# Entry of the experts' loop re-ordered, and two low parts of the first norm moved to VectorE, in a one-core DeltaNet, HGRN2 and PEER layer

## Chip, cores and metric

One Trainium2 chip, one core of it. The metric is the device time of one execution in microseconds (us). Three runs of the kernel before gave 2094.04, 2093.02 and 2092.74 us, a median of 2093.02.

## Reference

```
h = rmsnorm(x, norm1); proj = h @ w_in                  # x: 512 x 1024 float32
y_a = gated_delta(q, k, v, beta, alpha) ... @ w_branch_a
y_b = hgrn2(f, i, q) ... @ w_branch_b
x  = x + (sigmoid(g_a) * y_a + sigmoid(g_b) * y_b) @ w_out
h2 = rmsnorm(x, norm2)
s  = (h2 @ w_pq) . sub_keys; top 16 of each half; best 16 of the sums per head; gate = softmax
h  = gelu(h2 . expert_u[idx]); x = x + sum_k gate_k * h_k * expert_v[idx_k]     # 128 x 128 experts
out = rmsnorm(x, final_norm)
```

## The kernel before

Every float32 product is made of three: a matrix is split into a high part rounded for TensorE and a low part, the rest (`w_split`, L485: ScalarE copies `raw` into `hi`, and another engine computes `lo = raw - hi`), and high·high, high·low and low·high are added in PSUM. Weights come in units of 128 x 1024 float32 (512 KB) through a pool of three buffers for each of `wraw`, `whi` and `wlo`. `w_raw(n)` issues the load of unit n on SyncE's queue; `w_cut(n)` splits it. The argument `eng` says who computes the low part: VectorE (`vec`), GpSimd (`gps`), or, with `None`, ScalarE writes minus the high part and GpSimd issues a DMA that adds the raw data to it.

All instructions of an engine run in the order in which the program wrote them (`in_order`, L292), and each DMA queue takes its issues in that order too.

**The first norm (L1034 to L1093).** TensorE multiplies the unscaled x by units 0 to 4 while the norm is still being computed. Unit 1 (PSUM tile `poB`) is followed by unit 2 (`pl`), then by units 3 and 4 in turns (`pl`, `mm`). Beside unit 1, `squares(k)` squares one eighth of x on ScalarE and VectorE adds it into `acc` (L436). After two pieces of unit 2, `token_scales` (L441) sums `acc` over the partitions on TensorE (`mA`); VectorE forms `r` (L444) and GpSimd takes its power -1/2 (L445). `spread_scales` (L447) multiplies the identity by `r` on VectorE (`rd`, four 128 x 128 tiles) and spreads it with TensorE (`mC`). Then x is scaled and split again (`scaled`, `resplit`), and the next unit of TensorE needs the new `hhi` and `hlo`. A few small constants (`late_constants`, L351) are computed in between on VectorE and ScalarE.

**The experts' loop (L1785 to L1835).** Of the 128 x 128 experts, block i has 128. For tokens 0 to 367 all experts are computed densely: `u_mm` is the product with the block's u (24 products of 368 columns, `h` in PSUM; blocks 0 to 29 before the loop, the others in it), `u_act` the gelu into `slots`, and `y_mm(i)` adds gate · h · v into six PSUM banks (18 products, `y`). For the other tokens GpSimd gathers rows of u and v by index (`gather`, 128 rows of 1024 float32 each; five buffers), and VectorE consumes them. The dense gates lie in HBM as `gD`, written in slots of 32 tokens from `stage` (L1588); the last slot has 16 valid tokens, and of its 128 columns 16 are written there and the other 112 at L1807. `g_load(i)` (L1690) reads the gates of four blocks (768 KB) back into one of two buffers in `stage`; the second of them lies on the memory from which L1807 writes.

The loop runs i = -3, -2, ..., 127. Iteration i issues the loads of v and u of block i + 3 (`v_load`, L1702, and `w_load`, called at L1801), prepares block i + 1 (`prep`, L1717) and computes block i. `prep(m)` makes on VectorE `hg` (gate times slot, L1728), high parts `vh`, `wh`, then the split of the u block (`us`), then the low parts `wl` (L1741) and `vl` (L1742). `y_part` multiplies wh·vh, wh·vl, wl·vh in this order. At L1805 GpSimd copies one number of the first gates, so that the first gathers wait for them.

```
            if 0 < i + GLEAD < P:                     # L1793, GLEAD = 5, GB = 4
                g_load(i + GLEAD, nc.scalar)
            if n < NU:                                # L1800, n = i + 3
                uraw[n] = w_load(I["eut"][n + NPRE])
            if n == 0:
                g_load(0, nc.sync)
                gps.tensor_copy(cut(8512, 1), gbs[0][:, 0, 0, 0:1])
            if n == 1:
                nc.sync.dma_start(gD[NA - 1][:, 16:], gt[0][:, 16:])
```

Called with i = -1, `g_load(4, nc.scalar)` is thus issued on ScalarE's queue ahead of all work of `prep(0)`.

Of the kernel before, what the change touches and what calls it, by code (L numbers as in the profile page):

```python
# [22 lines left out]
P = 128  # L23
T = 512
D = 1024
DC = D // P
# [17 lines left out]
NPRE = 30  # L44
# [29 lines left out]
NDMA = 4  # L74
# [5 lines left out]
GLEAD = 5  # L80
LAG = 2
GB = 4
# [197 lines left out]
def build(ctx, tc, I, O):  # L280
# [199 lines left out]
    def w_load(src):  # L480
        raw = wpool.tile([P, DC, UW], F32, tag="wraw", name="wraw")
        nc.sync.dma_start(raw, src)
        return raw

    def w_split(raw, eng=gps):  # L485
        hi = wpool.tile([P, DC, UW], F32R, tag="whi", name="whi")
        lo = wpool.tile([P, DC, UW], F32R, tag="wlo", name="wlo")
        act(hi, raw, AF.Copy)
        if eng is None:

            act(lo, hi.bitcast(F32), AF.Copy, scale=-1.0)
            gps.dma_start(out=lo, in_=raw, accum_op=OP.add)
        else:
            eng.tensor_tensor(lo, raw, hi.bitcast(F32), OP.subtract)  # L494
        return hi, lo

    def w_raw(n):
        if n < len(order):
            kind, j = order[n]
            raws[n] = w_load(I["eut"][j] if kind == "u" else I["wu"][UNITS[kind, j]])  # L500

    def w_cut(n):
        if n < len(order):
            wts[n] = w_split(raws.pop(n), vec if n < 2 else gps if n < N0 + NDMA else None)

    def piece(p, w, c, m):
        whi, wlo = w
# [8 lines left out]
    with ExitStack() as ph:  # L516
# [534 lines left out]
        for k in range((NF - 1) * DC):  # L1051
# [6 lines left out]
            if k < DC:  # L1058
                squares(k)
            if k == 1:  # L1060
                w_cut(3)
                w_raw(4)
            if k >= LB:
                next(lbs, None)
            if k == SC1:
# [574 lines left out]
    with ExitStack() as ph:  # L1640
# [76 lines left out]
        def prep(m, between=None):  # L1717
# [16 lines left out]
            else:  # L1734
                act(vh, vr, AF.Copy)
                act(wh, hg, AF.Copy)
            if m < NU:
                us[m] = w_split(uraw.pop(m), vec)
            if between is not None:
                consume(between, rws.pop(between))  # L1740
            vec.tensor_tensor(wl, hg, wh.bitcast(F32), OP.subtract)  # L1741
            vec.tensor_tensor(vl, vr, vh.bitcast(F32), OP.subtract)  # L1742
            vs[m], ws[m] = (vh, vl), (wh, wl)


# [39 lines left out]
        for i in range(-LEAD, P):  # L1785
            n = i + LEAD
            if i == P - TAIL - 1:
# [2 lines left out]
                nc.sync.dma_start(fn, I["fnorm"].partition_broadcast(P))  # L1790
                for tt in (NT,) + tuple(range(NT)):
                    x_load(tt)
            if 0 < i + GLEAD < P:  # L1793
                g_load(i + GLEAD, nc.scalar)
            if n < P - TAIL:
                v_load(n)
            if i == P - TAIL - EARLY - 1:
                for k in range(P - TAIL, P):
                    v_load(k)
            if n < NU:  # L1800
                uraw[n] = w_load(I["eut"][n + NPRE])  # L1801
            if n == 0:
                g_load(0, nc.sync)

                gps.tensor_copy(cut(8512, 1), gbs[0][:, 0, 0, 0:1])  # L1805
            if n == 1:
                nc.sync.dma_start(gD[NA - 1][:, 16:], gt[0][:, 16:])  # L1807
            if i == 8:
                sx = junk[:, 0:P].bitcast(I32)
# [58 lines left out]
```

## Time and profile before

| | |
|---|---|
| median of three runs | 2093.02 us |
| the profiled execution's own time | 2093.28 us |
| its span, first to last instruction | 2091.1 us |
| busy: TensorE | 2012.5 us (96%) |
| busy: VectorE / ScalarE / GpSimd | 1511.8 / 940.7 / 857.3 us |
| mean granted clock of TensorE | 0.990 |

The span is 2.2 us shorter than the time of the same execution. The shares are means over the whole span; the two places of the change are 20 us long each, so they are read in the timeline: there a row gives start, duration, engine and line, tiles, count, and in brackets how long the engine had been idle and what ended that. A row that merges several instructions gives their stretch from the first start to the last end.

### The profile page before, as it was taken

How to read it: one execution, taken by the hardware profiler on the slowest of the kernel's cores; microseconds unless marked ns; L12 is line 12 of the kernel's file. 1: busy time of each engine (PE TensorE's matmuls, PEld its weight loads, DVE VectorE, ACT ScalarE, POOL GpSimd, SP SyncE). 2: the span in 40 equal slices, each digit the busy share in tenths (PEclk: the TensorE clock that was granted, in tenths of full speed). 3: DMA queues.
4: the chain of work that ended last, by engine and by line, in shares of the span. 5: the costliest groups of instructions: out<-in, count | busy, mean ns of one | idle time of the engine just before them, and what ended most of it. 6: DMA issues, size and time to landing. Idle time of an engine off the chain costs nothing.

```text
span 2091.1 us, 34918 instructions
## 1 busy us (share of the span) xinstructions
PE 2012.5 (96%) x13182; PEld 1729.2 (83%) x13182; DVE 1511.8 (72%) x2956; ACT 940.7 (45%) x1739; POOL 857.3 (41%) x863
## 2 busy tenths in 40 slices
PE   7899999999999999999798899999999999999998
PEld 5678787887878787888787799999999998898886
DVE  7666546656662366999996587787877878788887
ACT  4555555545554323566575333333333333333334
POOL 3566645655645644311101134334334433334522
PEclk9999999999999999999999999999999999999999
DMA  3322232132222543677799799999989989889996
GB/s 134 114 72 83 64 107 73 62 98 63 83 83 93 191 156 126 186 199 192 192 331 330 281 330 327 337 319 332 327 321 326 325 323 324 320 327 323 323 312 228
DMA packets 194873, 456.84 MB, mean 218 GB/s; under 512 B 28128, under 2 KB 91776, under 8 KB 193040
## 3 DMA queue, kind: packets, MB, share of 16 engines
q1 hardware_dynamic: 96016, 231.29, 31.0%
q0 software_dynamic: 47520, 173.04, 26.3%
q10 hardware_dynamic: 51168, 50.28, 7.3%
q8 instruction: 103, 1.69, 0.3%
q14 instruction: 66, 0.54, 0.1%
HBM read 393.11 MB, written 39.40 MB: 207 GB/s over the span
## 4 chain that ended last, share of the span: by engine, by line
PE 58%; DVE 14%; ACT 2%; issue 2%; DMA 2%; POOL 0%; SPq 0%; ACTq 0%; DVEq 0%; POOLq 0%
PE y L285 23%; PE h L285 19%; PE mm L285 12%; DVE Bg L1564 2%; DVE stage L1266 1%; DVE scr L1262 1%; DVE stage L1260 1%; DVE A L1560 1%; PE iv L285 1%; DMA gD<-stage 1%; DVE oh L1314 1%; PE pl L285 1%; DVE tv L1258 1%; DVE tv L1264 1%; PE mC L285 1%
## 5 line engine op out<-in xcount | busy, mean ns | idle before, releaser
L494 POOL TENSOR_TENSOR wlo<-wraw,whi 128x1024 fp32r<-128x1024 f32 x106 | 255.0, 2407 | 269.3 <-ACT whi L288 268.8
L285 PE MATMUL h<-hhi,wlo 128*128 128x368 f32 x1024 | 339.4, 331 | 6.2 <-DMA wlo<-wraw 6.2
L285 PE MATMUL h<-hhi,whi 128*128 128x368 f32 x1024 | 340.4, 332 | 2.0 <-ACT hext L288 1.9
L285 PE MATMUL h<-hlo,whi 128*128 128x368 f32 x1024 | 339.5, 332 | 1.6 <-POOL hlo L459 1.2
L285 PE MATMUL mm<-hhi,whi 128*128 128x512 f32 x792 | 328.8, 415 | 1.0 <-ACT a_k L288 0.6
L285 PE MATMUL mm<-hlo,whi 128*128 128x512 f32 x792 | 311.4, 393 | 4.2 <-POOL hlo L459 3.0
L288 ACT ACTIVATE whi<-wraw 128x1024 fp32r<-128x1024 f32 (+1 forms) x251 | 263.2, 1049 | 110.7 <-PE mm L285 46.1
L285 PE MATMUL mm<-hhi,wlo 128*128 128x512 f32 x792 | 309.6, 391 | 2.0 <-DMA wlo<-wraw 2.0
L285 PE MATMUL y<-vl,wh 128*128 128x512 f32 x756 | 297.7, 394 | 10.8 <-DVE vl L1742 10.5
L285 PE MATMUL y<-vh,wh 128*128 128x512 f32 x756 | 295.5, 391 | 4.8 <-DVE wh L1733 4.8
L285 PE MATMUL y<-vh,wl 128*128 128x512 f32 x756 | 296.5, 392 | 0.0
L1660 POOL DMA_INDIRECT row<-eu,eidx x144 | 172.6, 1199 | 285.5 <-DVE stage L1670 271.9
L1660 POOL DMA_INDIRECT row<-ev,eidx x144 | 174.9, 1215 | 275.0 <-DVE h2g L1678 219.0
L494 DVE TENSOR_TENSOR wlo<-wraw,whi 128x1024 fp32r<-128x1024 f32 x99 | 121.3, 1225 | 177.3 <-ACT whi L288 175.7
L285 PEld LDWEIGHTS h<-hhi,wlo 128*128 128x128 f32 x1024 | 193.7, 189 | 12.0 <-DMA wlo<-wraw 7.7
L285 PEld LDWEIGHTS h<-hhi,whi 128*128 128x128 f32 x1024 | 193.2, 189 | 6.9 <-ACT hext L288 2.5
L285 PEld LDWEIGHTS h<-hlo,whi 128*128 128x128 f32 x1024 | 193.3, 189 | 2.5 <-POOL hlo L459 1.8
L288 ACT ACTIVATE hext<-h 128x368 f32<-128x368 f32 x88 | 41.9, 476 | 334.6 <-PE h L285 329.3
L285 PEld LDWEIGHTS mm<-hlo,whi 128*128 128x128 f32 x792 | 148.7, 188 | 40.1 <-POOL hlo L459 4.7
L285 PEld LDWEIGHTS y<-vl,wh 128*128 128x128 f32 x756 | 142.3, 188 | 43.2 <-DVE vl L1742 16.2
L285 PEld LDWEIGHTS mm<-hhi,whi 128*128 128x128 f32 x792 | 149.0, 188 | 27.7 <-ACT a_k L288 1.0
L285 PEld LDWEIGHTS mm<-hhi,wlo 128*128 128x128 f32 x792 | 149.4, 189 | 26.5 <-DMA wlo<-wraw 2.3
(443 smaller groups left out, 3758.4 us busy)
## 6 DMA issues: line engine op xcount, KB each, us to landing
wraw<-eut SPq DMA_DIRECT2D x128, 512.0 KB
stage<-ev SPq DMA_DIRECT2D x126, 512.0 KB
wraw<-wu SPq DMA_DIRECT2D x119, 512.0 KB
stage<-gD ACTq DMA_DIRECT2D x31, 768.0 KB
gD<-stage ACTq DMA_DIRECT2D x11, 2048.0 KB
wlo<-wraw POOLq DMA_DIRECT2D x42, 512.0 KB
sg<-sgD SPq DMA_DIRECT2D x16, 256.0 KB
sgD<-tmpP SPq DMA_DIRECT2D x14, 256.0 KB
```

What stands on the lines that cost most here:

```text
L285: nc.tensor.matmul(o, l, r, start=start, stop=stop)
L288: nc.scalar.activation(o, i, f, **kw)
L494: eng.tensor_tensor(lo, raw, hi.bitcast(F32), OP.subtract)
L1258: vec.max(val[:, 0:8], src)
L1260: vec.max_index(idx[:, 0:8], val[:, 0:8], src)
L1262: vec.match_replace(scr, val[:, 0:8], src, -3.0e38)
L1264: vec.max(val[:, 8:16], scr)
L1266: vec.max_index(idx[:, 8:16], val[:, 8:16], scr)
L1314: eng.tensor_tensor(oh[:, :, 0:n, :], oh[:, :, 0:n, :], oh[:, :, n:2 * n, :], OP.add)
L1560: vec.tensor_tensor(A, it[:, 0, t0:t0 + TB].rearrange("p (n u) -> p n u", u=2)[:, :, None, :].to_broadcast([P, TP, P, 2]), iov[:, None, :, ...
L1564: vec.tensor_tensor(Bg[:, q].rearrange("p n a b u -> p (n a) b u"), hi[:, p1:p1 + TP].rearrange("p n a u -> p (n a) u")[:, :, None, :].to_ ...
L1660: gps.indirect_dma_start(out=r, out_offset=None, in_=I["eu" if k < NK else "ev"], in_offset=bass.IndirectOffsetOnAxis(ap=at, axis=0))
```

## The change

At the start, the low part of unit 2 goes from GpSimd to VectorE; the split of unit 3 moves behind all eight squares and its low part to VectorE too. The last unit before the loop (the u block 29) has its low part computed by VectorE in place of ScalarE's copy and GpSimd's adding DMA. At the loop's entry, the first gates are loaded ahead of the first u block; GpSimd's copy writes into `gg2` instead of `stage`; the rest of the last gate slot is written one iteration later; `g_load(4)` is issued in iteration 1 instead of iteration -1; and in `prep(0)` the split of the u block stands behind `wl` and `vl`.

```
-            wts[n] = w_split(raws.pop(n), vec if n < 2 else gps if n < N0 + NDMA else None)
+            wts[n] = w_split(raws.pop(n), vec if n < 4 or n == len(order) - 1 else gps if n < N0 + NDMA else None)
...
             if k == 1:
+                w_raw(4)
+            if k == DC:
+
                 w_cut(3)
-                w_raw(4)
...
-            if m < NU:
+            if 0 < m < NU:
                 us[m] = w_split(uraw.pop(m), vec)
             if between is not None:
                 consume(between, rws.pop(between))
             vec.tensor_tensor(wl, hg, wh.bitcast(F32), OP.subtract)
             vec.tensor_tensor(vl, vr, vh.bitcast(F32), OP.subtract)
+            if m == 0:
+
+                us[m] = w_split(uraw.pop(m), vec)
...
-            if 0 < i + GLEAD < P:
+            if i == 1:
+                g_load(GB, nc.scalar)
+            elif GB < i + GLEAD < P:
                 g_load(i + GLEAD, nc.scalar)
...
+            if n == 0:
+                g_load(0, nc.sync)
+
+                gps.tensor_copy(gg2[:, 0:1], gbs[0][:, 0, 0, 0:1])
             if n < NU:
                 uraw[n] = w_load(I["eut"][n + NPRE])
-            if n == 0:
-                g_load(0, nc.sync)
-
-                gps.tensor_copy(cut(8512, 1), gbs[0][:, 0, 0, 0:1])
-            if n == 1:
+            if n == 2:
+
                 nc.sync.dma_start(gD[NA - 1][:, 16:], gt[0][:, 16:])
```

TensorE's instructions and their order are the same in both kernels. VectorE in the first norm, from the low part of unit 1 on (`wlo` low parts, `acc` the sums of squares, `mx` and `e` constants, `r` the scales), before:

```order
L494 TENSOR_TENSOR wlo<-wraw,whi 128x1024
L436 TENSOR_TENSOR acc<-acc,sq 128x512 x7
L355 TENSOR_TENSOR mx<-vecs 128x8
L356 TENSOR_TENSOR e_287<-vecs,mx 128x8
L357 TENSOR_TENSOR e_288<-vecs,mx 128x8
L444 TENSOR_SCALAR r_120<-mA 128x4
```

and now:

```order
L494 TENSOR_TENSOR wlo<-wraw,whi 128x1024 x2
L436 TENSOR_TENSOR acc<-acc,sq 128x512 x7
L494 TENSOR_TENSOR wlo<-wraw,whi 128x1024
L355 TENSOR_TENSOR mx<-vecs 128x8
L356 TENSOR_TENSOR e_287<-vecs,mx 128x8
L357 TENSOR_TENSOR e_288<-vecs,mx 128x8
L444 TENSOR_SCALAR r_120<-mA 128x4
```

One low part more stands ahead of the seven sums and one behind them, ahead of the constants and of `r`.

SyncE's queue at the loop's entry (`stage<-ev` a v block, `wraw<-eut` a u block, `stage<-gD` the first gates, `gD<-stage` the rest of the last gate slot), before:

```order
L1702 DMA stage<-ev 128x1024
L482 DMA wraw<-eut 128x1024
L1693 DMA stage<-gD 128x12x128
L1702 DMA stage<-ev 128x1024
L482 DMA wraw<-eut 128x1024
L1807 DMA gD<-stage 128x3584
L1702 DMA stage<-ev 128x1024
L482 DMA wraw<-eut 128x1024
```

and now:

```order
L1704 DMA stage<-ev 128x1024
L1695 DMA stage<-gD 128x12x128
L482 DMA wraw<-eut 128x1024
L1704 DMA stage<-ev 128x1024
L482 DMA wraw<-eut 128x1024
L1704 DMA stage<-ev 128x1024
L482 DMA wraw<-eut 128x1024
L1815 DMA gD<-stage 128x3584
```

The gates are second instead of third, and the write is behind the third pair of blocks instead of the second.

ScalarE there (`ogA<-h` and `hext<-h` gelus of u blocks, `whi` high parts of u blocks, `stage<-gD` the gates of blocks 4 to 7), before:

```order
L288 ACTIVATE ogA<-h 128x368 x4
L1693 DMA stage<-gD 128x12x128
L288 ACTIVATE whi<-wraw 128x1024
L288 ACTIVATE vh<-stage 128x1024
L288 ACTIVATE wh<-hg 128x384
L288 ACTIVATE whi<-wraw 128x1024
L288 ACTIVATE hext<-h 128x368
L288 ACTIVATE vh<-stage 128x1024
```

and now:

```order
L288 ACTIVATE ogA<-h 128x368 x4
L288 ACTIVATE whi<-wraw 128x1024
L288 ACTIVATE vh<-stage 128x1024
L288 ACTIVATE wh<-hg 128x384
L288 ACTIVATE whi<-wraw 128x1024
L1695 DMA stage<-gD 128x12x128
L288 ACTIVATE hext<-h 128x368
L288 ACTIVATE vh<-stage 128x1024
```

The load of the second gates has moved behind the high parts of u blocks 0 and 1 and of v block 1; it now stands ahead of the first gelu of the loop and of v block 2.

## Rows read from the trace of the kernel before

**Rows 1.** The page, busy time and share of the span by engine.
```profile
PE 2012.5 (96%) x13182; PEld 1729.2 (83%) x13182; DVE 1511.8 (72%) x2956; ACT 940.7 (45%) x1739; POOL 857.3 (41%) x863
```

**Rows 2.** Timeline of VectorE, first norm: start, duration (us), engine, line, tiles.
```profile
15.12 1.22 DVE L494 TENSOR_TENSOR wlo<-wraw,whi 128x1024 fp32r<-128x1024 f32 x1 [1.00 <-ACT whi L288]
17.45 4.80 DVE L436 TENSOR_TENSOR acc<-acc,sq 128x512 f32<-128x512 f32 x2 [1.11 <-ACT sq L288]
24.75 1.49 DVE L436 TENSOR_TENSOR acc<-acc,sq 128x512 f32<-128x512 f32 x2
26.16 0.16 DVE L355 TENSOR_TENSOR mx<-vecs 128x8 f32<-128x8 f32 x1
...
27.50 0.16 DVE L444 TENSOR_SCALAR r<-mA 128x4 f32<-128x4 f32 x1 [0.91 <-PE mA L285]
...
28.80 2.98 DVE L450 TENSOR_SCALAR rd<-ident,r 128x128 f32<-128x128 f32 x4
```

**Rows 3.** Timeline of GpSimd, first norm.
```profile
16.46 5.24 POOL L494 TENSOR_TENSOR wlo<-wraw,whi 128x1024 fp32r<-128x1024 f32 x2 [13.78 <-ACT whi L288]
27.74 1.02 POOL L445 TENSOR_TENSOR r<-r,mhalf 128x4 f32<-128x4 f32 x1 [6.04 <-DVE mx L363]
28.73 2.39 POOL L494 TENSOR_TENSOR wlo<-wraw,whi 128x1024 fp32r<-128x1024 f32 x1
```

**Rows 4.** Timeline of ScalarE, first norm: the high part of unit 4.
```profile
26.86 1.04 ACT L288 ACTIVATE whi<-wraw 128x1024 fp32r<-128x1024 f32 x1
```

**Rows 5.** Timeline of TensorE, first norm.
```profile
26.29 1.17 PE L285 MATMUL mA<-ones,acc 128*128 128x2 f32 x8 [3.01 <-DVE acc L436]
...
46.97 0.49 PE L285 MATMUL mm<-hlo,whi 128*128 128x512 f32 x1 [0.66 <-DVE hlo L459]
```

**Rows 6.** Waits of TensorE from 1165 us to the end: us in total, times, longest.
```profile
PE y L285 <- DVE vl L1742: 1.0, 1, 1.0
```

**Rows 7.** Timeline of TensorE, the loop's entry: second product of block 0, first of block 2.
```profile
1157.30 0.79 PE L285 MATMUL y<-vl,wh 128*128 128x512 f32 x1 [9.52 <-DVE vl L1742]
...
1174.82 0.39 PE L285 MATMUL y<-vh,wh 128*128 128x512 f32 x1
```

**Rows 8.** Timeline of SyncE's queue at the entry.
```profile
1136.64 0.40 SPq L1693 DMA_DIRECT2D stage<-gD  x1
...
1146.07 0.33 SPq L1807 DMA_DIRECT2D gD<-stage  x1
```

**Rows 9.** Timeline of VectorE at the entry; the last row is of block 2.
```profile
1145.44 0.56 DVE L1728 TENSOR_TENSOR hg<-hext,stage 128x384 f32<-128x384 f32 x1 [16.84 <-DMA stage<-gD]
...
1146.52 0.35 DVE L1733 CAST wh<-hg 128x384 fp32r<-128x384 f32 x1
...
1156.03 1.22 DVE L1742 TENSOR_TENSOR vl<-stage,vh 128x1024 fp32r<-128x1024 f32 x1
...
1171.33 1.22 DVE L1742 TENSOR_TENSOR vl<-stage,vh 128x1024 fp32r<-128x1024 f32 x1
```

**Rows 10.** Timeline of ScalarE and its queue at the entry.
```profile
1152.90 0.38 ACTq L1693 DMA_DIRECT2D stage<-gD  x1
1153.33 1.06 ACT L288 ACTIVATE whi<-wraw 128x1024 fp32r<-128x1024 f32 x1 [10.56 <-DMA gD<-stage]
...
1166.90 0.48 ACT L288 ACTIVATE hext<-h 128x368 f32<-128x368 f32 x1 [7.69 <-PE h L285]
```

**Rows 11.** DMA queues, 1146 to 1153 us: packets, MB, share; an issue's size.
```profile
q0 software_dynamic: 8, 0.03, 1.1%
...
gD<-stage SPq DMA_DIRECT2D x1, 1792.0 KB
```

**Rows 12.** DMA queues, 1153 to 1158 us.
```profile
q0 software_dynamic: 331, 1.22, 60.8%
```

**Rows 13.** Busy time by stretch; the last three columns: granted clock, DMA share, GB/s.
```profile
1137.60:1145.10 7.50, 4.23 (x24) 3.80 (x23) 0.00 (x0) 0.95 (x2) 0.00 (x0) 1.00 0.98 345
...
1152.80:1158.50 5.70, 1.20 (x3) 1.01 (x4) 3.30 (x4) 2.75 (x4) 0.00 (x0) 0.50 1.03 411
```

## The prediction

> **What bounds the kernel now.** The page first: TensorE is busy for 96% of the span [rows 1], so time can only come out of the few places where it stands still or runs at its lower clock. The table of its waits from 1165 us to the end has one line, 1.0 us in all [rows 6]: once the experts' loop runs, TensorE sets the pace, and whatever its start is moved by, the end is moved by. That leaves the two places of the change, which are read in the timeline engine by engine.
>
> In the first norm TensorE has done two pieces of unit 2 and then stands for 3.01 us until the sum of squares `acc` is complete at 26.24 [rows 2, 5]. The reader is to see why it is late: the first two of the seven sums take 4.80 us together, the last two 1.49 [rows 2], and in the stretch of the first two GpSimd runs the low parts of units 2 and 3, 5.24 us from 16.46 [rows 3]. The sums wait for GpSimd. Behind them comes a chain: `r`, its power on GpSimd, the four `rd`, the spread scales, the scaled x and its new split. At 46.97 TensorE waits for that chain again [rows 5]. So this place is bound by the chain behind the last square, not by TensorE.
>
> At the loop's entry TensorE waits 9.52 us for `vl` of block 0 and goes on only at 1157.30 [rows 7]. Going back: `vl` starts at 1156.03 [rows 9], behind the low part of u block 0, which needs the high part that ScalarE makes at 1153.33, after 10.56 us of idleness that a write to `gD` ended: ScalarE's queue had the load of the second gates (1152.90) ahead of it, and that waited for the rest of the last gate slot to be written [rows 10], a write of 1792 KB [rows 11] issued at 1146.07 [rows 8]. Independently, `hg` starts at 1145.44, when the first gates have landed [rows 9].
>
> **The sum, part by part.** The parts of the first norm go together. The low part of unit 2 can start on VectorE when it did on GpSimd, at 16.46 [rows 3], and takes 1.22 [rows 2], to 17.68. The seven sums then have no GpSimd beside them: two in 1.49 [rows 2] make at least 0.75 each, 5.2 for seven, and 5.5 if the pace from one to the next is 0.8 (an estimate, for each needs the one before); I take 5.5, to 23.2 instead of 26.24. The low part of unit 3 follows, 1.22, to 24.4. The first constant starts there instead of at 26.16 [rows 2], and ScalarE's exponentials and high part of unit 4, which wait for it, come as much earlier, so that high part ends near 26.86 + 1.04 - 1.77 = 26.13 [rows 4]. TensorE reached its wait at 26.29 - 3.01 = 23.28, so `acc` no longer holds it; `r` can follow at about 24.5 and its power, 1.02, ends before 26. GpSimd then starts the low part of unit 4 at 26.2, where it started at 28.73 [rows 3]: 2.5 us earlier. The four `rd` take 2.98 us because they lie beside this low part [rows 2, 3], and do so again. Operations that don't need each other overlap a little, which makes the 2.5 rather more, and 3.3 (the sums' own gain at 0.75 each) is the other end. I take **2.7 us**. TensorE now waits for `rd` instead, some 2 us; that is cover and costs nothing, because the chain ends later anyway. The later split of unit 3 costs nothing either: it is used only after all of unit 2, some 24 products behind.
>
> The low part of u block 29 is 1.22 on a VectorE that is idle for 16.84 us there [rows 9]; ScalarE and GpSimd lose a copy and a DMA. Nothing on the path: TensorE reaches the entry a little earlier and waits there. If the entry were no longer late, this would be worth a few tenths.
>
> The gates of blocks 0 to 3: 768 KB (0.79 MB), now behind one block of 0.52 MB instead of two. In 1137.60 to 1145.10 the queues moved 345 GB/s [rows 13]. One block less is 1.5 us, so `hg` at 1143.9; the bytes alone, 1.31 MB from 1137.6, would be there at 1141.4. I take 1143.2, 2.2 us earlier. The high parts `vh` and `wh` end 1.43 later (1146.87 - 1145.44, [rows 9]), `wl` takes about half a us, `vl` 1.22: with the u block's split out of the way `vl` ends at 1146.35, and TensorE goes on there instead of at 1157.30, **10.9 us** earlier. From 1157.30 to block 2 at 1174.82 it took 17.5 us [rows 7], part of it at the lower clock (0.50 to 1158.5, [rows 13]); after a wait of nearly 5 us I leave that in. So block 2 would start at 1163.9.
>
> What is late next is the load of the second gates, in front of the gelu and the high part of v block 2 on ScalarE. It still waits for the 1792 KB (1.84 MB) write, now behind seven loads, 3.93 MB. Once it is issued, ScalarE goes on 0.43 later, and from that gelu to the end of `vl` of block 2 it is 1171.33 + 1.22 - 1166.90 = 5.65 [rows 9, 10]: 6.1 together. TensorE needs this `vl` at 1164.1, so the write must have landed by 1158.0. Bounds: SyncE's queue alone, 5.77 MB from 1137.6 at 345 GB/s, lands at 1154.3; with all five gathers ahead (2.62 MB, now free to start when the gates land), the 5.80 MB left at 1145.1 at the 411 GB/s that both kinds reached together [rows 13] land at 1159.2. While the write ran in the kernel before, the gathers moved only 0.03 MB [rows 11], and beside 512 KB loads they took 60.8% [rows 12]; so I count the three gathers that can get ahead of it: 4.75 MB, 1156.7. That leaves a margin of 1.3 us and no wait.
>
> By the Trainium skill, DMA: Bandwidth & Descriptors (Queues, rings and completion order), each DMA engine goes round the queues and drains a whole packet of one before it turns to the next. The 0.03 MB of [rows 11] agree only if the write counts as one packet per engine; turn by turn in equal pieces, the write would share with all five gathers and land at the late bound, and the sum would be 1.2 us less.
>
> Sum: 2.7 + 10.9 = 13.6. Against the profiled execution's own 2093.28 us this gives **2079.7 us**. That execution is 0.26 us above the median of the three runs.
>
> **Rivals.** (a) *The write lands late.* At 1159.2 `vl` of block 2 ends at 1165.3, 1.2 us after TensorE wants it: 2080.9. For it: five gathers start with the gates. Against: [rows 11].
>
> (b) *`rd` ahead of the low part of unit 4.* By the sum GpSimd starts at 26.2, and VectorE is through with the constants at nearly the same moment. If VectorE is first, the four `rd` don't wait out the 2.39 us [rows 3], and about 2.3 more are gained: 2077.4. Against: in the rows GpSimd is first by 0.07 us, and both move alike. The Trainium skill, SBUF — State Buffer (Who interferes with whom), says that whoever issues first keeps the shared port for its whole instruction. The 2.98 us of [rows 2] agree for one order; no row here shows the other.
>
> (c) *The gates land early*, at 1141.8, with GpSimd's adding DMA gone: 1.4 more, if the write also lands by 1156.5: 2078.3.
>
> (d) *The start's gain doesn't arrive*, so that the change does not do there what it seems to: the new wait for `rd`, with the lower clock it may bring, makes TensorE and not the chain the late one, or a later stage that does not move swallows it: 2093.28 - 10.9 = 2082.4. Against: [rows 5], the wait at 46.97.
>
> (e) *More at the entry is late*: gates at 1143.9, a wait in block 2 with another stretch at the lower clock: 8 at the entry, 2083 to 2085.
>
> (f) *Slower.* The second gates' load holds ScalarE's queue, and with it every gelu and v block, until the write lands. Price: each us that it lands after 1158 is a us. Zero gain overall is reached at 1158.0 + 13.6 = 1171.6, and 0.2% slower (4.2 us) at 1176. For that the 8.4 MB since 1137.6 would have to move at 218 GB/s, which gives 2097.5, where the rows have 345 and 411 [rows 13]. Only a queue that stops would do this.
>
> **How the numbers follow.** Forecast 0.47; (a) 0.15, (b) 0.10, (c) 0.10, (d) 0.10, (e) 0.05, (f) 0.03. The range, 2076.2 to 2084.5, takes in all but (f), part of (e), and sums of (b) and (c) with each other; it is 2 in 10 or less that is left out. 0.2% is 4.2 us, about what a measurement of this kernel can tell from no change. All cases but (f) are faster by more than that: faster 0.95; same 0.02, what is left between (e) and (f); slower 0.03.
>
> **What would show it.** In the profile after: seven sums in about 5.5 us, ended near 23.2, and no wait for them on TensorE; a new wait of about 2 us for `rd`; the wait of 46.97 near 44.3. At the entry: `hg` at its old place less the start's 2.7 and another 2.2; `vl` right behind `wl`; TensorE's wait there about 5 us instead of some 14; no wait of TensorE in block 2; the second gates' issue 19 to 20 us after the first load begins to move. Wrong would be a wait for `vl` of block 2 longer than 2 us, a first stretch that ends less than 2 us earlier, or new waits in the loop behind block 3, which would mean that the transfers and not TensorE set its pace.

## The result, and the profile after

The changed kernel takes 2077.11 us (median of six runs, 2076.30 to 2080.05) where the kernel before takes 2093.28 us (six runs beside them, 2092.33 to 2094.37): a ratio of 0.9924 with a 95% interval from 0.9912 to 0.9937, faster by 16.2 us or 0.76%. The forecast was 2079.7 us, with a range from 2076.2 to 2084.5. Five further runs in another series gave 2079.99 us against 2093.63 us, 0.9937 [0.9924, 0.9951]. So the gain is 14 to 16 us, and single executions of the changed kernel lie between 2076.3 and 2082.4 us. The profiled execution took 2077.48 us (span 2075.7 us, granted clock 0.993).

The page says little, as it should: TensorE's busy time is what it was [rows 1], and the span is shorter.

```profile
PE 2013.0 (97%) x13182; PEld 1731.3 (83%) x13182; DVE 1511.5 (73%) x2959; ACT 939.6 (45%) x1738; POOL 850.9 (41%) x860
```

**The first norm**, timeline of VectorE, GpSimd, ScalarE and TensorE after, one engine behind the other (start, duration in us, engine, line, tiles, and in brackets the idle time before and what ended it):

```profile
17.14 5.46 DVE L436 TENSOR_TENSOR acc<-acc,sq 128x512 f32<-128x512 f32 x7
22.52 1.22 DVE L494 TENSOR_TENSOR wlo<-wraw,whi 128x1024 fp32r<-128x1024 f32 x1
25.59 2.95 DVE L450 TENSOR_SCALAR rd<-ident,r 128x128 f32<-128x128 f32 x4
...
25.48 2.40 POOL L494 TENSOR_TENSOR wlo<-wraw,whi 128x1024 fp32r<-128x1024 f32 x1 [0.21 <-ACT whi L288]
...
29.72 0.60 ACT L288 ACTIVATE tmpB<-mC 128x512 f32<-128x512 f32 x1 [4.32 <-PE mC L285]
...
28.01 1.67 PE L285 MATMUL mC<-rd,onesm 128*128 128x128 f32 x8 [2.13 <-DVE rd L450]
...
29.91 0.63 PE L285 MATMUL pl<-hhi,wlo 128*128 128x512 f32 x1
...
54.56 0.51 PE L285 MATMUL mm<-hlo,whi 128*128 128x512 f32 x1 [0.52 <-POOL hlo L459]
```

The seven sums run without a gap and end at 22.60, where the last of them ended at 26.24 [rows 2]; TensorE's wait of 3.01 us for them [rows 5] is gone. In its place stands a wait of 2.13 us for `rd`, whose four instructions still take 2.95 us beside the low part of unit 4 on GpSimd, and behind it a stretch in which a product takes 0.63 us (TensorE at the lower of its two levels, 1.2 instead of 2.4 GHz; the granted clock is 0.50 from 29 to 31 us). The product that waited at 46.97 [rows 5] starts at 44.46, and the chain of the scaled x holds TensorE until 54.56. The same two ends of that chain in the trace of before, ScalarE's first reading of the spread scales and TensorE's last wait:

```profile
32.45 0.60 ACT L288 ACTIVATE tmpB<-mC 128x512 f32<-128x512 f32 x1 [4.54 <-PE mC L285]
...
57.29 0.49 PE L285 MATMUL mm<-hlo,whi 128*128 128x512 f32 x1 [0.51 <-POOL hlo L459]
```

From the one to the other it is 24.84 us before and after, so what the spread scales gain is what the end of the chain gains: 2.73 us. The four `rd`, however, ended 3.24 us earlier (28.54 instead of 31.78). The half microsecond between the two is lost in the eight products of `mC`, which stand in this chain: behind the wait for `rd` they take 1.67 us, at a granted clock of 0.74 from 28 to 29 us. In e4, e5 and e6 below, TensorE waits as long for `rd`, the granted clock stays at 1.00, and they take 1.16. The line of e5:

```profile
28.63 1.16 PE L285 MATMUL mC<-rd,onesm 128*128 128x128 f32 x8 [2.14 <-DVE rd L450]
```

So TensorE's standing costs nothing by itself, but the lower level behind it does.

**The entry**, the same view: SyncE's queue, GpSimd, VectorE, ScalarE and TensorE after, each in order of time:

```profile
1131.29 0.33 SPq L1704 DMA_DIRECT2D stage<-ev  x1
1131.99 0.38 SPq L1695 DMA_DIRECT2D stage<-gD  x1
...
1135.36 0.48 SPq L1815 DMA_DIRECT2D gD<-stage  x1
...
1138.20 0.60 POOL L1810 COPY gg<-stage 128x1 f32<-128x1 f32 x1 [17.68 <-DMA stage<-gD]
...
1138.20 0.56 DVE L1730 TENSOR_TENSOR hg<-hext,stage 128x384 f32<-128x384 f32 x1 [8.60 <-PE h L285]
...
1140.14 1.22 DVE L1744 TENSOR_TENSOR vl<-stage,vh 128x1024 fp32r<-128x1024 f32 x1
...
1155.52 1.22 DVE L1744 TENSOR_TENSOR vl<-stage,vh 128x1024 fp32r<-128x1024 f32 x1
...
1150.65 0.38 ACTq L1695 DMA_DIRECT2D stage<-gD  x1
1151.09 0.48 ACT L288 ACTIVATE hext<-h 128x368 f32<-128x368 f32 x1 [6.63 <-PE h L285]
...
1139.78 0.47 PE L285 MATMUL y<-vh,wh 128*128 128x512 f32 x1 [1.50 <-DVE wh L1735]
1141.41 0.80 PE L285 MATMUL y<-vl,wh 128*128 128x512 f32 x1 [1.17 <-DVE vl L1744]
...
1159.01 0.39 PE L285 MATMUL y<-vh,wh 128*128 128x512 f32 x1
```

`vl` of block 0 now starts at 1140.14 instead of 1156.03 [rows 9], and TensorE's wait for it is 1.17 us instead of 9.52 [rows 7]. `hg` and GpSimd's copy, which waits for the gates alone, start together at 1138.20, so it is the gates that released `hg`, although its row names TensorE. The load of the second gates went out at 1150.65, when the write had landed; `vl` of block 2 was done at 1156.74, and TensorE, which began block 2 at 1159.01, did not wait for it. Behind 1165 us there is the same single wait as before [rows 6] (waits of TensorE: us in total, times, longest):

```profile
PE y L285 <- DVE vl L1744: 1.0, 1, 1.0
```

**Where the 16 us came from.** TensorE executes the same products in the same order in all kernels of this text, so the start of a product in one trace can be taken from its start in another. This gives, against the trace of before (negative is earlier):

| stretch of the trace of before | after: us |
|---|---|
| to 15.4 (input loads, not part of the change) | -0.41 |
| 15.4 to 58.1 (first norm) | -2.31 |
| 58.1 to 1129 | -0.21 |
| 1129 to 1170.2 (u block 29, entry, blocks 0 and 1) | -12.88 |
| 1170.2 to 2080.1 | -0.51 |

### The profile page after: what moved, and what is told of

Read it like the earlier page. It is cut to its first block, busy times and chain, and to the rows that moved or that the text cites. A ratio compares the mean times of both kernels' runs of the same rounds, so it can differ in the third digit from the quotient of the medians.

```text
span 2075.7 us, 34910 instructions
## 1 busy us (share of the span) xinstructions
PE 2013.0 (97%) x13182; PEld 1731.3 (83%) x13182; DVE 1511.5 (73%) x2959; ACT 939.6 (45%) x1738; POOL 850.9 (41%) x860
## 4 chain that ended last, share of the span: by engine, by line
PE 52%; DVE 13%; issue 2%; DMA 1%; ACT 1%; POOL 0%; DVEq 0%; POOLq 0%; SPq 0%; ACTq 0%
PE y L285 24%; PE h L285 19%; PE mm L285 8%; DVE Bg L1566 2%; DVE stage L1268 1%; DVE scr L1264 1%; DVE stage L1262 1%; DVE A L1562 1%; DVE oh L1316 1%; DVE tv L1260 1%; DVE tv L1266 1%; DVE oh L1311 0%; PE g L285 0%; DVE oh L1306 0%; DMA row<-x2D 0%
## 5 line engine op out<-in xcount | busy, mean ns | idle before, releaser
L494 POOL TENSOR_TENSOR wlo<-wraw,whi 128x1024 fp32r<-128x1024 f32 x104 | 249.7, 2401 | 256.3 <-ACT whi L288 255.8
```

## Experiments

Twelve runs were made. Medians are given as the difference to the kernel before in the same series (before: 2093.30 for the first four runs, 2094.34 for the next four, 2093.63 for e9 to e11, 2093.39 for e12). Executions of one kernel differ by some us, and so do medians of two series of the same kernel (e2 and e10 by 3.5 us, after and e9 by 2.5). By the medians alone e5, e6 and e7 can therefore not be told from the changed kernel, and e11 and e12 not from e8; what is said of them is read from one trace of each. All numbers of this table are differences of starts in the timeline, in us. "u29" is the distance between the two products around block 29's low part, "first y" the one from the last product of block 29 to the first of block 0, "vl" the one from there to the second product of block 0, "blocks" from that product to the first of block 2; "gates" is the time from the issue of v block 0's load to GpSimd's copy, which waits for the first gates; "norm" the shift of the first norm against before, as in the table above.

| run | norm | gates | u29 | first y | vl | blocks | median to before |
|---|---|---|---|---|---|---|---|
| before | 0 | 10.39 | 0.75 | 5.10 | 10.28 | 17.52 | 0 |
| after | -2.31 | 6.91 | 0.17 | 1.83 | 1.64 | 17.59 | -16.17 |
| e1 start only | -1.94 | 9.65 | 1.31 | 3.15 | 10.27 | 17.78 | -3.75 |
| e2 entry only | +1.14 | 7.04 | 0.17 | 1.97 | 1.64 | 18.82 | -9.65 |
| e3 second gates only | -0.07 | 9.35 | 1.06 | 3.74 | 2.64 | 18.40 | -7.83 |
| e4 second gates, write at old places | -2.83 | 6.19 | 0.17 | 1.60 | 1.64 | 22.39 | -10.95 |
| e5 first gates at old place | -2.80 | 8.63 | 0.17 | 3.67 | 1.64 | 17.58 | -13.70 |
| e6 split of u first | -2.79 | 6.45 | 0.17 | 1.74 | 4.13 | 18.67 | -12.88 |
| e7 block 29 by DMA | -2.49 | 8.89 | 1.48 | 2.28 | 1.64 | 16.10 | -14.75 |
| e8 `rd` first | -4.89 | 7.52 | 0.17 | 2.40 | 1.64 | 17.46 | -18.64 |
| e9 after again | -1.83 | 6.84 | 0.17 | 1.59 | 1.64 | 17.71 | -13.64 |
| e10 entry only again | -0.22 | 6.92 | 0.17 | 1.82 | 1.64 | 17.73 | -13.15 |
| e11 `rd` and v first | -4.94 | 6.70 | 0.17 | 0.83 | 0.31 | 16.11 | -18.83 |
| e12 and write earlier | -4.90 | 6.95 | 0.17 | 1.38 | 0.31 | 16.09 | -20.06 |

**e1, the start alone** (from the kernel before):

```
-            wts[n] = w_split(raws.pop(n), vec if n < 2 else ...)
+            wts[n] = w_split(raws.pop(n), vec if n < 4 else ...)
             if k == 1:
-                w_cut(3)
                 w_raw(4)
+            if k == DC:
+                w_cut(3)
```

> The kernel before with the first norm's part of the change alone (units 2 and 3's low parts on VectorE, unit 3's split behind the last square); block 29 and the experts' entry stay as they were. Theory (the chain behind the squares ends earlier and the gain reaches the end): the trace of the changed kernel has TensorE's last wait for the first norm 2.7 us earlier, of which 0.4 lies in earlier input loads, so 2.3 to 2.8 us off 2093.3: 2090.5 to 2091. Rival (a later stage swallows it, and the 16 us all come from the entry): no difference that can be measured, 2093.3, within 0.5.

Measured: 2089.55 us, 3.75 less than before (0.9983 [0.9974, 0.9992]). In the trace the first norm gives 1.94; another 1.5 lie at the entry, which this kernel does not change, and 0.8 are lost in between. The rival falls: the start's gain is real and most of it arrives. From the medians its size is known only as 1.7 to 5.4 us.

**e2 and e10, the entry alone** (from the changed kernel):

```
-            ... vec if n < 4 or n == len(order) - 1 else ...
+            ... vec if n < 2 or n == len(order) - 1 else ...
             if k == 1:
+                w_cut(3)
                 w_raw(4)
-            if k == DC:
-                w_cut(3)
```

> The changed kernel with the first norm as before; block 29's low part on VectorE and the whole entry (gates ahead of u block 0, order of the splits, second gates and write later) stay. Theory (start and entry add up): 16.2 us less the start's 2.3 to 2.8, so about 13.5 below the kernel before, 2079.6 to 2080.7. Rival (the start decides nothing, or what it gives is lost in the wait at the entry): the same time as the changed kernel, 2077.1.

Measured: 2083.65 us (2079.72 to 2084.22), outside both expectations. Its profiled execution had 15 products of 0.43 us instead of 0.23 between 60 and 960 us (2.9 us; the changed kernel's had 8, the one of before none) and 5 more than usual behind the wait at the entry (1.0 us). So it was run again, with the changed kernel (e9) beside it:

> The changed kernel with the first norm as before, once more: its first five runs had a median of 2083.65 (2079.72 to 2084.22), where start and entry as a sum ask for 2079.6 to 2080.7, and its profiled execution had two extra stretches of TensorE at its lower level (about 10 products at 0.43 instead of 0.23 us, some 2 us each). Theory (start and entry add up; those stretches come and go between executions): beside the changed kernel on the same chip, 2.3 to 2.8 us behind it, about 2079.5 to 2080. Rival (the parts don't add up: without the start's gain the entry loses another 3 us): 5 us or more behind it, 2082.5 to 2084.

> The changed kernel unaltered, as the base on this chip for the two runs beside it. Same as before: 2077.1, within 1.5 us.

Measured: 2080.48 us for the entry alone and 2079.99 for the changed kernel. The 2083.65 was not a property of the kernel. But the medians of this series show only half a us between the two, less than the theory asks, and the changed kernel itself came out nearly 3 us worse than in the first series. Medians of five runs do not resolve 2.4 us here. The traces do: the seven profiled executions that have the changed kernel's first norm (after, e1, e4 to e7, e9) show -1.83 to -2.83, the four with the old one (before, e2, e3, e10) -0.22 to +1.14. Of the seven, the three in which `mC` takes 1.16 us (e4, e5, e6) show -2.79 to -2.83; where it takes 1.47, 1.67 and 2.08 us (e7, after, e1), the shift is smaller by as much. (e9, whose granted clock was 0.50 already from 15.8 to 19.2 us, shows -1.83.)

**e3, only the second gates' load moved** (from the kernel before):

```
-            if 0 < i + GLEAD < P:
+            if i == 1:
+                g_load(GB, nc.scalar)
+            elif GB < i + GLEAD < P:
                 g_load(i + GLEAD, nc.scalar)
```

> The kernel before with one edit: the load of the second gates (gate blocks 4 to 7) is issued with block 1, behind the high part of u block 0 on ScalarE, and no longer ahead of it. Gates and write stay where they were. Theory (this load, waiting for the 1792 KB write in front of ScalarE's queue, is the larger part of the late entry): the high part of u block 0 comes when its block lands, about 1142, all VectorE work of block 0 is done 1 to 3 us behind the high parts that end at 1146.9, so vl of block 0 ends at 1149 to 1150 where it ended at 1157.3: 7 to 8 us off, 2085.5 to 2086.5. Rival (the gates' landing and the order of the splits are the cause): under 3 us, 2090 or more.

Measured: 2085.47 us, 0.9963 [0.9950, 0.9977], as the theory had it. In the timeline of TensorE the wait for `vl` shrinks from 9.52 us [rows 7] to

```profile
1148.95 0.79 PE L285 MATMUL y<-vl,wh 128*128 128x512 f32 x1 [2.17 <-DVE vl L1742]
```

which is 7.64 us less between the two products (10.28 to 2.64). This one moved load is more than half of the entry's gain.

**e4, the reverse: all but that** (from the changed kernel; the load of the second gates and the write at their old places):

```
-            if i == 1:
-                g_load(GB, nc.scalar)
-            elif GB < i + GLEAD < P:
+            if 0 < i + GLEAD < P:
                 g_load(i + GLEAD, nc.scalar)
...
-            if n == 2:
+            if n == 1:
                 nc.sync.dma_start(gD[NA - 1][:, 16:], gt[0][:, 16:])
```

> The changed kernel, but the second gates' load is issued at its old place, ahead of everything of block 0 on ScalarE, and the rest of the last gate slot is written with block 1 again (its old place in SyncE's queue). Theory (the load holds ScalarE until the write has landed): ScalarE makes no high part of blocks 0 and 1 until the write lands, and vl of block 0 with it; since the first high parts vh and wh of block 0 would also stand behind that load, vl comes no earlier than in the kernel before, so most of the entry's 12 us are gone: 2086 to 2090, slower than with the second gates alone moved. If vh and wh are ahead of the load in ScalarE's queue, then vl of block 0 comes as in the changed kernel and only u block 0's split and hext are late: 2079.5 to 2082. Rival (the second gates' place is worth nothing): 2077.1.

Measured: 2082.35 us, in the milder of the two cases. The first case overlooked that block 0's high parts `vh` and `wh` are made on VectorE, not on ScalarE, so `vl` came as early as in the changed kernel. What is held is u block 0. The timeline of ScalarE and its queue, then TensorE, in this kernel:

```profile
1147.22 0.38 ACTq L1695 DMA_DIRECT2D stage<-gD  x1
1147.65 1.06 ACT L288 ACTIVATE whi<-wraw 128x1024 fp32r<-128x1024 f32 x1 [9.03 <-DMA gD<-stage]
...
1148.76 0.44 PE L285 MATMUL h<-hhi,whi 128*128 128x368 f32 x1 [3.59 <-ACT whi L288]
1150.02 0.68 PE L285 MATMUL h<-hhi,wlo 128*128 128x368 f32 x1 [0.82 <-DVE wlo L494]
```

ScalarE stands 9.03 us with the load ahead of it, until the write has landed, and TensorE waits 4.4 us in the middle of block 0 and runs on at its lower level (granted clock 0.50 from 1149.7 to 1153; "blocks" 22.39). The order of the splits and the place of the load belong together: with the load ahead and the split first, as before, it was `vl` that stood behind the write.

**e5, the first gates behind u block 0 again** (from the changed kernel):

```
+            if n < NU:
+                uraw[n] = w_load(I["eut"][n + NPRE])
             if n == 0:
                 g_load(0, nc.sync)
                 gps.tensor_copy(gg2[:, 0:1], gbs[0][:, 0, 0, 0:1])
-            if n < NU:
-                uraw[n] = w_load(I["eut"][n + NPRE])
```

> The changed kernel with the first gates' load put back behind the load of u block 0 on SyncE's queue (the touch by GpSimd with it). Theory (hg comes when the bytes ahead of the gates and the gates themselves have landed): one block of 0.52 MB more ahead of them, at 345 GB/s 1.5 us, so hg, vl and TensorE 1.5 us later: 2078.6. If hg moved by 3.3 us because of this place alone: 2080.4. Rival (TensorE is held by something else at the entry): 2077.1.

Measured: 2080.64 us. The gates take 8.63 us instead of 6.91, and TensorE's first y comes 3.67 instead of 1.83 us behind block 29: 1.7 to 1.8 us, near the 1.5 of one block at 345 GB/s. So the place in the queue is only half of the 3.3 us that the first y gained.

**e6, the split of u block 0 ahead of the low parts again** (from the changed kernel):

```
-            if 0 < m < NU:
+            if m < NU:
                 us[m] = w_split(uraw.pop(m), vec)
...
-            if m == 0:
-                us[m] = w_split(uraw.pop(m), vec)
```

> The changed kernel with the split of u block 0 ahead of the low parts wl and vl of block 0 again. Theory (VectorE's order decides only what its own operation costs, since the high part is there by then): TensorE's wait for vl is longer by one low part, 1.2 us, or up to 2.1 if the high part on ScalarE, at 1139.50 in the changed kernel and 1.05 long, ends behind wh: 2078.3 to 2079.2. Rival (the order of the splits is the main part of the entry's gain): 2085 or more. Rival (no part): 2077.1.

Measured: 2081.46 us; the second product comes 4.13 instead of 1.64 us behind the first, 2.5 us more, above what was expected. The timeline of VectorE in this kernel shows why:

```profile
1140.14 0.35 DVE L1735 CAST wh<-hg 128x384 fp32r<-128x384 f32 x1
1141.89 1.22 DVE L494 TENSOR_TENSOR wlo<-wraw,whi 128x1024 fp32r<-128x1024 f32 x1 [1.40 <-ACT whi L288]
```

It stands 1.40 us for the high part on ScalarE, for u block 0 now lands behind the gates, and then spends 1.22 us on the low part. The new order of the splits is needed all the more because the gates were moved ahead of the block.

**e7, block 29's low part by DMA again** (from the changed kernel):

```
-            ... vec if n < 4 or n == len(order) - 1 else ...
+            ... vec if n < 4 else ...
```

> The changed kernel with the low part of block 29 made by GpSimd's adding DMA again, as before. The shift of TensorE's products between the two traces grew by 0.6 us there. Theory of the prediction (nothing on the path, TensorE waits at the entry): 2077.1, within 0.5. Rival A (the 0.6 us are real and reach the end): 2077.7. Rival B (the adding DMA of 0.5 MB lies ahead of the gates in the queues and accounts for the rest of hg's 3.3 us): hg 1 to 1.5 us later, 2078.1 to 2078.6.

Measured: 2079.59 us. TensorE waits for this low part, and the gates land later (timeline of TensorE and GpSimd in this kernel):

```profile
1135.46 0.44 PE L285 MATMUL h<-hhi,wlo 128*128 128x368 f32 x1 [1.15 <-DMA wlo<-wraw]
...
1139.95 0.61 POOL L1810 COPY gg<-stage 128x1 f32<-128x1 f32 x1 [9.48 <-DMA stage<-gD]
```

That is 8.89 us from v block 0's issue instead of 6.91. What lies ahead of the gates on the DMA engines can be seen in the DMA queues of this kernel (1131 to 1136 us: packets, MB, share of 16 engines; q0 has the adding DMA, q1 SyncE's loads):

```profile
q0 software_dynamic: 144, 0.52, 69.7%
q1 hardware_dynamic: 296, 0.59, 30.8%
```

u29, first y and vl add up to 5.40 us against 3.64, so 1.8 us are lost ahead of block 0. In the profiled execution 1.5 of them came back ("blocks" 16.10), because TensorE did not fall to its lower level behind the wait this time (granted clock 1.00 from 1135 to 1170). By this trace both rivals hold, the second by more than it said.

**e8, unit 4's low part behind `rd`, on VectorE** (from the changed kernel):

```
-            ... vec if n < 4 or n == len(order) - 1 else ...
+            ... vec if n < 5 or n == len(order) - 1 else ...
             if k == SC1:
                 token_scales(sums)
-                w_cut(4)
                 w_raw(5)
             if k == SC2:
                 spread_scales(r, sb)
+                w_cut(4)
```

> The changed kernel with the low part of unit 4 on VectorE too, behind the four rd and the spread scales, so that GpSimd runs nothing beside the four rd. Theory (rd take 2.95 us only because GpSimd's low part holds them back, and the chain behind them sets TensorE's waits for hlo): rd in about 0.8 us, 2.1 earlier, TensorE's wait for rd gone or below 0.3 and no half-speed stretch behind it, the waits for hlo 2.1 earlier: 2074.5 to 2075.0. Rival (TensorE, the spread scales or unit 4's low part on VectorE in the chain of the scaled x become the late one): less than 1 us, 2076.2 to 2077.1, or slower by the 1.2 us that VectorE now does in between: 2078.3.

Measured: 2075.70 us, 0.9909 [0.9894, 0.9924], below the changed kernel's two series, with intervals that touch. The timeline of VectorE and TensorE in the first norm of this kernel:

```profile
25.48 0.87 DVE L450 TENSOR_SCALAR rd<-ident,r 128x128 f32<-128x128 f32 x4
26.27 1.22 DVE L494 TENSOR_TENSOR wlo<-wraw,whi 128x1024 fp32r<-128x1024 f32 x1
...
25.82 1.16 PE L285 MATMUL mC<-rd,onesm 128*128 128x128 f32 x8
...
51.85 0.50 PE L285 MATMUL mm<-hlo,whi 128*128 128x512 f32 x1 [0.52 <-POOL hlo L459]
```

With nothing on GpSimd the four `rd` take 0.87 us where they took 2.95, `mC` follows without a wait and at the full clock, and the last wait of the chain stands at 51.85 instead of 54.56. The first norm's shift is -4.89, and -4.94 and -4.90 in the two later kernels with this edit: 2.5 us beyond the mean of -2.4 of the seven, and 2.1 beyond the three of them in which the granted clock did not fall in `mC`. From ScalarE's first reading of `mC` to the last wait it is 24.84 us here too.

**e11, v block 0 split ahead of `hg`** (e8 and this edit):

```
+            if m == 0:
+                vec.tensor_copy(vh, vr)
+                vec.tensor_tensor(vl, vr, vh.bitcast(F32), OP.subtract)
             vec.tensor_tensor(hg..., OP.mult)
             if m == 0:
-                vec.tensor_copy(vh, vr)
                 vec.tensor_copy(wh, hg)
```

(and `vl` of block 0 left out where it stood).

> The kernel with unit 4's low part behind the rd on VectorE, and at the entry the split of v block 0 (vh and vl) ahead of hg on VectorE, which is idle there until the gates land. Theory (TensorE's two waits at the entry are the path from the gates' landing: hg, vh, wh, then wl and vl): wh ends 0.6 earlier, and TensorE goes from the first product to the second without the 1.2 us wait, at most 0.2 for wl: 1.6 to 2.0 below the 2075.7 of the kernel without this edit, 2073.7 to 2074.1; up to 1.5 more if the shorter standing leaves TensorE at its higher level behind it. Rival (v block 0 lands no earlier than the gates, or the next wait, for the high part of v block 1, takes the gain): 2075 to 2075.7.

Measured: 2074.80 us, no more below the kernel before than e8 (18.83 us against 18.64). At the entry the theory was right: first y and vl are 0.83 and 0.31 us where e8 has 2.40 and 1.64, TensorE stays at its full clock (granted 1.00 from 1130 to 1170; "blocks" 16.11), and at block 2 it is 4.2 us earlier than in e8, counted from 1129 us of the trace of before. But 2.8 of them are given back, in waits that none of the kernels above has. The timeline of this kernel, TensorE at blocks 2 and 4, ScalarE ahead of the first, VectorE ahead of the second:

```profile
1155.74 0.50 PE L285 MATMUL y<-vl,wh 128*128 128x512 f32 x1 [1.21 <-DVE vl L1746]
...
1172.83 0.50 PE L285 MATMUL y<-vl,wh 128*128 128x512 f32 x1 [0.59 <-DVE vl L1746]
...
1150.04 0.48 ACT L288 ACTIVATE hext<-h 128x368 f32<-128x368 f32 x1 [7.80 <-DMA gD<-stage]
...
1166.64 0.56 DVE L1733 TENSOR_TENSOR hg<-hext,stage 128x384 f32<-128x384 f32 x1 [3.76 <-DMA stage<-gD]
```

This is the write that the prediction named as late next, and behind it the second gates themselves.

**e12, the write one block earlier** (e11 and this edit):

```
-            if n == 2:
+            if n == 1:
                 nc.sync.dma_start(gD[NA - 1][:, 16:], gt[0][:, 16:])
```

> The same kernel as in the run with v block 0's split ahead of hg, with the rest of the last gate slot written one block earlier in SyncE's queue (behind the loads of block 1, ahead of those of block 2). In that run TensorE's entry came 4.2 us earlier than without the edit, and 2.8 of them were lost again in waits for vl of block 2 (behind the second gates' load, issued when the write had landed at 1149.6, then gelu, high part and low parts) and of block 4 (behind the second gates' own landing, 1166.6). Theory (the write is what is late next): it lands 2.5 to 3 us earlier, both waits go or shrink to a few tenths, and 2 to 2.8 us are gained: about 2072. Rival (v block 2, now behind the write, is late instead and takes its place): vl of block 2 no earlier, only the wait at block 4 gone, 2073.8 to 2074.8.

Measured: 2073.33 us, 20.06 less than before, 0.9903 [0.9886, 0.9919]: the lowest median of all. The second gates are issued at 1144.95 instead of 1149.61, the wait at block 2 is gone, and of TensorE's waits behind block 1 one of 1.0 us, which the kernel before has too, and one of 0.3 are left. ScalarE at the gelu of block 0, and TensorE, in the timeline of this kernel:

```profile
1145.85 0.48 ACT L288 ACTIVATE hext<-h 128x368 f32<-128x368 f32 x1 [3.97 <-PE h L285]
...
1170.97 0.50 PE L285 MATMUL y<-vl,wh 128*128 128x512 f32 x1 [0.30 <-DVE vl L1746]
```

The gelu waits for TensorE again and no longer for the write. Of the 2 to 2.8 us expected, the trace shows 1.5 (0.83 us given back behind block 1 instead of 2.36). Between 1129 and 1170.2 this execution gained 1.7 us less than e11's, 1.2 of it ahead of block 0, where the two kernels do the same, and the intervals of e11 (0.9894 to 0.9924) and e12 overlap. That the waits are gone is shown; that e12 is the faster of the two is likely and no more. The step of the change that moved this write one iteration later thus earned nothing in this kernel. Alone, in the changed kernel, it was not tried, nor was the copy of GpSimd into `gg2`.

## Why the prediction was right, point by point

**The chain behind the squares (2.7 us).** Right in mechanism and nearly in size. The seven sums took 5.46 us (5.5 forecast); the wait for `acc` went, and a wait of 2.13 us for `rd` came (2 forecast). That it "costs nothing" holds for the standing, not for what follows it: `rd` ended 3.24 us earlier, and 0.51 of that was lost in `mC` at the lower level. The first norm's gain was 2.31 in this trace, 1.8 to 2.8 in seven, and 2.8 where the level did not fall. Rival (d), that it would not arrive, falls with e1.

**Rival (b), `rd` ahead of unit 4's low part.** It did not happen by itself: GpSimd was first again, by 0.11 us (25.48 against 25.59). e8 made it happen, and it was worth 2.5 us against the mean of the seven, 2.1 against those without the fall in `mC`, where the prediction priced it at 2.3. The Trainium skill, SBUF — State Buffer (Who interferes with whom), lets the operation that comes first keep the port which VectorE and GpSimd share until it ends. The 2.95 us beside GpSimd and the 0.87 us alone agree.

**Block 29's low part (nothing).** Wrong, and the largest miss. "Nothing on the path" overlooked two things. TensorE did wait for the adding DMA, 0.42 to 1.15 us in the four traces that have it (before, e1, e3, e7). And that DMA's 512 KB were under way ahead of the first gates: e7 shows 8.89 us instead of 6.91 from v block 0's issue to the gates. Rival (c) had this effect at 1.4 us; it is 2.0 in the landing and 1.8 in what TensorE waits. It was not a rival but a part of the likeliest case.

**The first gates (2.2 us).** Right in direction, and the term that was too small: `hg` came 7.2 us earlier (1145.44 to 1138.20), of which 2.9 are what the trace was ahead at 1129, so 4.3 in the prediction's own terms. TensorE's two waits at the entry were 1.50 and 1.17 us, 2.7 together, where about 5 was named as a sign. The first y gained 3.3. With the gates' place alone put back (e5) 1.7 to 1.8 are lost, so the term for the order was right to half a us; the rest is the adding DMA.

**`vl` right behind `wl` (8.7 of the 10.9 us).** Right: the distance between block 0's first two products fell from 10.28 to 1.64, by 8.64. e3 gives 7.64 of them to the second gates' load alone, and the new order of the splits gives the last 1.0, as 10.28, 2.64 and 1.64 show. e6 shows that the same order is worth 2.5 when the gates lie ahead of the u block.

**No wait in block 2.** Right, but the step to it was wrong. The forecast counted three gathers, 1.57 MB, ahead of the write and had it land 19.1 us after v block 0's load begins to move (1137.6 to 1156.7); by SyncE's queue alone it was 16.7. In the changed kernel the first bytes of that load move at 1132.2 and the second gates are issued at 1150.65, 18.4 us later, where 19 to 20 were named as a sign. In this time SyncE's queue moved 6.09 MB and the gathers 0.86 MB:

```profile
q1 hardware_dynamic: 2639, 6.09, 90.5%
q0 software_dynamic: 227, 0.86, 11.4%
```

(DMA queues of the changed kernel, 1132.2 to 1150.65 us: packets, MB, share of 16 engines; q1 has SyncE's loads and the write, q0 the gathers.) The write thus landed between the early bound and the forecast, with little more than half of the counted bytes of the gathers ahead of it. The reading of [rows 11] behind that step, a write that keeps the gathers out as one packet per engine, was wrong as well. Two us in the middle of the write:

```profile
q1 hardware_dynamic: 48, 0.69, 80.2%
q0 software_dynamic: 46, 0.19, 22.9%
```

(the same view, 1145 to 1147 us.) Write and gathers take turns packet by packet, 48 to 46, but a packet of the write is 14 KB and one of a gather 4 KB, so the write keeps nearly four fifths of the bytes. This is the rule of the Trainium skill, DMA: Bandwidth & Descriptors (Queues, rings and completion order), a whole packet of one queue and then the next; the trace agrees with it, and the prediction misread the row as speaking against it. Why then did the gathers move only 0.03 MB beside the write in the kernel before? Because they had not begun: from 1146 to 1152 us its DMA queues have no packet of the gathers at all. The first gather's bytes moved 4.4 to 5.3 us behind its issue in eleven traces and 6.2 to 6.5 in the three in which the write began to move within a us of that issue (before, e1, e3; before it was issued at 1146.35 and moved its first bytes behind 1152.5). What takes this long, and whether the write holds it back, was not tried.

**The margin.** The forecast left 1.3 us between the write and a wait in block 2. After, `vl` of block 2 ends at 1156.74 and its product starts at 1159.23, 2.5 us later. e11 used this up, and the wait appeared where the prediction had put it (rival (a) and (f) in small).

**The sum.** 13.6 forecast; 16.2 in the first series's medians, 13.6 in the second's, 15.8 in the profiled execution's own time. By the trace (2.3 in the norm, 12.9 at the entry against 10.9) the forecast was short by about 2 us, all of it in the gates' term and most of it from block 29's DMA. That the second series meets 13.6 is luck: two terms were off, the first norm's a little too large and the gates' 2 us too small, and single executions differ by as much.

## What to carry to other kernels

A DMA that waits for another DMA should be issued from a queue on which nothing is due: placed ahead of an engine's work, it puts everything behind it behind the transfer it waits for (7.6 us here for one line). Where a GpSimd operation lies beside VectorE operations on the path, move it behind them or to VectorE itself: one that nobody needed yet cost 2.1 to 2.6 us here. And cost the removal of a transfer not only by who waits for it but by what lies behind it in time on the same DMA engines: 512 KB taken out ahead of the gates were worth as much as moving 512 KB behind them.

## What was not expected of the hardware

TensorE's clock adds a scatter of its own. Behind the wait at the entry, block 0's products from the second to the last took 5.3 to 5.7 us in seven traces, 6.3 to 6.7 in three (e2, e3, e6) and 4.0 in e4, e7, e11 and e12; in these four the granted clock stayed at 1.00 there, although in e4 and e7 TensorE had stood for `vl` for the same 1.17 us as in the changed kernel, where it was 0.50 from 1141.3 to 1144.6. The first norm shows the same: behind a wait of 2.1 us for `rd` the level fell in after, e1 and e7 and did not in e4, e5 and e6. In the middle of the program, where nothing differs, 7 to 9 products ran at 0.43 instead of 0.23 us (in the changed kernel at a granted clock of 0.50 from 854.6 to 857.8) in ten of the fourteen profiled executions, 15 in one, and at most one in three, before among them (some 1.5 us for 8 products). A difference of 2 us between two single executions can be nothing more than this.

The gathers' start, 4.4 to 6.5 us behind their issue, and the division of the DMA engines by packets and not by bytes stand above; the second decides how much a large write with large packets takes from small transfers beside it.
